# The output projection's weights: split during the input projection, kept in DRAM, loaded into place

## The chip, the cores and the metric

The kernel runs on one core of a Trainium2 chip. The metric is the device time of one execution in microseconds (us). The version before was run three times: 1436.47, 1436.74 and 1441.49 us, median 1436.74 us. The trace used here is of a further, profiled execution.

## The reference

One decoder layer in float32 on 1024 tokens of width 1024. The mixer projects the normalised tokens with one wide matrix `w_in`, runs sparse attention on part of the columns and a short convolution on another, normalises both results, concatenates them and multiplies by one matrix `w_out`. Cross-attention into 256 memory tokens and a SwiGLU block follow. Cut to the part at issue:

```python
def hybrid_mixer(h, w_in, w_out, gn_nsa, gn_conv, conv_w, rel_bias, ...):
    proj = h @ w_in
    q, kc, vc, ks, vs, kw, vw, gl, cb, cc, cx = jnp.split(proj, IN_SPLITS, axis=-1)
    ...
    o_nsa = nsa_attention(q, kc, vc, ks, vs, kw, vw, gates, ...)   # (S, 512)
    u = cc * cx
    y = sum(conv_w[k] * u_pad[:, CONV_K - 1 - k: CONV_K - 1 - k + S] for k in range(CONV_K))
    o_conv = cb * y                                                # (S, 512)
    merged = jnp.concatenate([rmsnorm(o_nsa, gn_nsa), rmsnorm(o_conv, gn_conv)], axis=-1)
    return merged @ w_out                                          # w_out: (1024, 1024)
```

## The kernel before

Every float32 matrix product is made of three products of float32r operands: a number is split into hi (its copy in float32r, written by ScalarE) and lo (the rest, a subtraction on VectorE or GpSimd), and `mm3` (lines 122 to 125) issues hi x hi, hi x lo and lo x hi.

The work runs in stages. **Input projection** (to about 306 us of the trace): `proj_t` takes 128 columns of `w_in` at a time. SyncE loads them (`wr`), ScalarE writes `wh`, GpSimd writes `wl`, both double-buffered, and TensorE makes 48 matmuls of 512 columns. Beside it `prep_step` (line 298) prepares four pieces of the cross-attention's weights, one call per projection: it loads a piece into the only `praw` tile, splits it into `phl` (two tiles) on ScalarE and VectorE, and lets GpSimd store the result to DRAM one call later. After the sixth projection `mem_norm` uses the same tiles. **Attention** (306 to 577 us): 32 tasks of two heads. The scores of a task go through VectorE (minimum and bias), ScalarE (exponentials) and GpSimd (weights times gates) and come back to TensorE as transposes and products. Between them stand 16 `fill` units, which multiply the convolution's half by rows 512 to 1023 of `w_out` (tiles `wos[4]` to `wos[7]`). **Middle** (577 to about 800 us): `u_proj` multiplies the attention's half by rows 0 to 511 (`wos[0]` to `wos[3]`), then come the norms and the cross-attention. The SwiGLU block follows.

`load_wo(k)` (line 196) fills `wos[k]`, 128 rows of `w_out` as hi and lo, in one of the six tiles named `big`: two loads of 256 KB into `wraw`, and for each half a copy on ScalarE and a subtraction on VectorE. For k below 4 the attention's norm gain (`cols`, 12 + k) is multiplied in by lines 205 and 206. It is called for 4 to 7 ahead of the last projection, for 0 and 1 at tasks 9 and 21, and for 2 and 3 behind the attention.

A scheduler with a timing model of its own places each instruction in its engine's order; the order is then fixed, and an engine works it off without overtaking. So a call's place in the program is not its place on the engines. SyncE issues DMAs on one queue, GpSimd on another.

Of the kernel before, what the change touches and what calls it, by code (L numbers as in the profile page):

```python
# [9 lines left out]
F32 = mybir.dt.float32  # L10
F32R = mybir.dt.float32r
AF = mybir.ActivationFunctionType
OP = mybir.AluOpType
# [53 lines left out]
def hymba_kernel(ctx: ExitStack, tc: tile.TileContext, a, out: bass.AP):  # L67
# [9 lines left out]
    def f(t):  # L77
        return t.bitcast(F32)

    def dram(name, shape, dt=F32):  # L80
        return dpool.tile(shape, dt, name=name)
# [88 lines left out]
    wq_d = [dram(f"wq_d{c}", [P, 2, D], F32R) for c in range(2)]  # L170
    wm_d = [dram(f"wm_d{k}", [P, 2, D], F32R) for k in range(2)]
    km_d = dram("km_d", [P, 2, MH, MEMN], F32R)
    vm_d = dram("vm_d", [P, 2, MH, P], F32R)
# [17 lines left out]
    def big_tile():  # L191
        return big.tile([P, 4, 512], F32, name="big")

    wos, wraw = {}, [None]

    def load_wo(k):
        wos[k] = t = big_tile().bitcast(F32R)
        for n in range(2):
            raw = wraw[0].tile([P, 512], F32, name="wraw")
            Y.dma_start(raw, a["w_out"][0, k * P:(k + 1) * P, n * 512:(n + 1) * 512])  # L200
            if k >= 4:
                split(t[:, n, :], t[:, 2 + n, :], raw, V)
            else:
                col = cols[:, 12 + k:13 + k]
                A.activation(t[:, n, :], raw, AF.Copy, scale=col)
                V.scalar_tensor_tensor(t[:, 2 + n, :], raw, col, f(t[:, n, :]), op0=OP.mult, op1=OP.subtract)


    with ExitStack() as st:
# [82 lines left out]
        for k in range(2):  # L292
            prep_q.append((a["mem_wq"][0, :, k * P:(k + 1) * P].rearrange("(k p) c -> p k c", p=P),
                           [cols[:, 20 + c:21 + c] for c in range(KT)], wq_d[k]))
            prep_q.append((a["mem_wo"][0, k * P:(k + 1) * P, :], None, wm_d[k]))
        prep_live, prep_done = [], []

# [23 lines left out]
        def proj_t(c0, post):  # L321
            wh, wl = load_w(wst, w_in[0, :, c0:c0 + P])
            prep_step()
            pss = [pmm.tile([P, 512], F32, name="mm") for _ in range(2)]
            for k in range(KT):
                for n in range(2):
                    tok = slice(n * 512, (n + 1) * 512)
                    mm3(pss[n], wh[:, k, :], wl[:, k, :], hh[:, k, tok], hl[:, k, tok], k == 0, k == KT - 1)
            for n in range(2):
                post(n, pss[n], slice(n * 512, (n + 1) * 512))  # L330
# [55 lines left out]
        with ExitStack() as s2:  # L386
            cp = pool(s2, "conv", side="right")
            for c in range(4):
# [18 lines left out]
                if c == 3:  # L407
                    mem_tr()
                proj_t(C_CX + c * P, post_cx)
                V.tensor_scalar(y, u[:, 2:S + 2], cols[:, c:c + 1], None, op0=OP.mult)  # L410
# [21 lines left out]

        mem_kv()
        conv_stat()
        prep_stack.close()
# [11 lines left out]

        wraw[0] = pool(st, "wr", bufs=2, side="right")

# [112 lines left out]

        for k in (4, 5):
            load_wo(k)
        for k in (6, 7):
            load_wo(k)
        proj_k("s", C_KS)


    wraw[0] = ap2 = pool(at_stack, "ap2", bufs=2)  # L570
    with ExitStack() as st:
# [57 lines left out]
        def soft_stage(n, i, h0, qi, mb, nt):  # L629
# [58 lines left out]
            for j in range(2):  # L688
                (V if i < 0 else Gp).tensor_scalar(psel[:, j, :W], psel[:, j, :W], sm[:, 0, j:j + 1], 1.0, op0=OP.mult, op1=OP.mult)
            soft[n] = psel, pwin, w0  # L690
# [91 lines left out]
        for n, (i, h0) in enumerate(tasks):  # L782
# [9 lines left out]
            for _ in ahead:  # L792
                pass
            if n in (9, 21):
                load_wo(int(n == 21))
            if h0 == H - 2:
# [8 lines left out]
        for m in range(FILL[NT], 2 * NT):  # L805
            fill(m)
        load_wo(2)
        load_wo(3)
        wq = []
# [615 lines left out]
```

## Time and profile before

| | |
|---|---|
| median of three runs | 1436.74 us |
| profiled execution, its own time | 1439.82 us |
| its span in the trace | 1438.0 us |
| TensorE (PE) busy | 1352.8 us, 94% |
| VectorE (DVE) busy | 946.9 us, 66% |
| ScalarE (ACT) busy | 683.7 us, 48% |
| GpSimd (POOL) busy | 488.5 us, 34% |
| mean granted TensorE clock | 0.976 |

PE is busy nearly all the time, so a change shows in the time where PE waits, or where its clock is granted at half. A timeline row gives start, length, engine, line, instruction, tiles, and in brackets how long the engine had been idle and what it waited for. PEclk is the granted clock: 1.00 is 2.4 GHz, 0.50 is 1.2 GHz.

### The profile page before, as it was taken

Reading aid. Unit: us, or ns where it says so; the run is one execution under the profiler, and the core shown is the slowest. Engines: PE = TensorE matmul, PEld = TensorE weight load, DVE = VectorE, ACT = ScalarE, POOL = GpSimd, SP = SyncE. Lnnn points to the kernel's source line nnn. Section 1 sums busy time; section 2 is a strip of 40 time slices with the busy share of each in tenths; the row PEclk is TensorE's granted clock in tenths of the full one; section 3 lists DMA queues with packets and bytes.
Section 4 is the critical chain, followed back from the end, with each engine's and each line's share of the span. In section 5 each row is a group of like instructions: output and inputs, shape, how many; then the busy total and the mean of one; then the engine's idle time right before and its main releaser. Section 6 shows DMA issues by size and latency. Waiting matters only on the chain.

```text
span 1438.0 us, 19770 instructions
## 1 busy us (share of the span) xinstructions
PE 1352.8 (94%) x6748; PEld 1127.4 (78%) x6748; DVE 946.9 (66%) x2079; ACT 683.7 (48%) x1473; POOL 488.5 (34%) x456
## 2 busy tenths in 40 slices
PE   8999999989999998898779789999999999989997
PEld 6988888878988897686658568888888887867885
DVE  6454543456899995478876786555544544898787
ACT  5432242437877796345775432333333333444463
POOL 1222231217767563111120666644445441000000
PEclk9999999989999999899989999999999999999999
DMA  7572266394633203843236455432222225930213
GB/s 227 153 239 76 74 217 203 117 184 101 113 66 67 45 8 131 315 152 100 107 96 214 123 152 166 145 119 80 89 84 85 81 88 206 378 112 30 67 59 118
DMA packets 159909, 186.50 MB, mean 130 GB/s; under 512 B 8402, under 2 KB 115070, under 8 KB 157599
## 3 DMA queue, kind: packets, MB, share of 16 engines
q1 hardware_dynamic: 129568, 146.44, 31.8%
q0 software_dynamic: 29088, 36.70, 10.5%
q10 hardware_dynamic: 1152, 2.10, 0.4%
q8 instruction: 53, 0.87, 0.3%
q14 instruction: 48, 0.39, 0.1%
HBM read 130.16 MB, written 55.05 MB: 129 GB/s over the span
## 4 chain that ended last, share of the span: by engine, by line
PE 43%; DVE 5%; issue 2%; ACT 0%; POOL 0%; DVEq 0%
PE m L125 13%; PE m L124 13%; PE m L123 13%; DVE al L120 1%; PE s L123 1%; PE s L124 1%; PE s L125 1%; DVE bl L120 1%; DVE big L120 0%; DVE q L1339 0%; PE o L125 0%; DVE T2l L120 0%; PE o L123 0%; DVE cb L1328 0%; PE o L124 0%
## 5 line engine op out<-in xcount | busy, mean ns | idle before, releaser
L119 ACT ACTIVATE ah<-raw 128x512 fp32r<-128x512 f32 x132 | 83.1, 631 | 209.1 <-PE m L124 192.5
L123 PE MATMUL mm<-hh,wh 128*128 128x512 f32 x320 | 125.8, 393 | 0.0
L124 PE MATMUL mm<-hl,wh 128*128 128x512 f32 x320 | 125.3, 392 | 0.0
L125 PE MATMUL mm<-hh,wl 128*128 128x512 f32 x320 | 124.8, 392 | 0.0
L120 DVE TENSOR_TENSOR al<-raw,ah 128x512 fp32r<-128x512 f32 x118 | 104.1, 884 | 25.8 <-ACT ah L119 25.6
L120 POOL TENSOR_TENSOR wl<-wr,wh 128x1024 fp32r<-128x1024 f32 x22 | 55.6, 2530 | 160.7 <-ACT wh L119 160.6
L124 PE MATMUL m<-bl,ah 128*128 128x512 f32 x264 | 102.8, 395 | 4.0 <-DVE bl L120 4.0
L125 PE MATMUL m<-bh,al 128*128 128x512 f32 x264 | 101.0, 393 | 4.8 <-DVE al L120 4.8
L1162 POOL TENSOR_TENSOR sg<-sg,tmp 128x512 f32<-128x512 f32 x44 | 66.0, 1501 | 82.5 <-DVE tmp L1161 39.5
L124 PE MATMUL m<-big,ah 128*128 128x512 f32 x232 | 92.0, 397 | 0.0
L120 DVE TENSOR_TENSOR ptl<-t,pth 128x512 fp32r<-128x512 f32 (+1 forms) x120 | 77.2, 655 | 11.7 <-ACT pth L119 11.5
L123 PE MATMUL m<-bh,ah 128*128 128x512 f32 x264 | 72.2, 390 | 1.1 <-ACT bh L119 1.1
L119 ACT ACTIVATE pth<-t 128x512 fp32r<-128x512 f32 (+1 forms) x120 | 66.5, 572 | 14.1 <-PE t L712 13.1
L125 PEld LDWEIGHTS mm<-hh,wl 128*128 128x128 f32 x320 | 60.5, 189 | 12.8 <-POOL wl L120 0.3
L123 PEld LDWEIGHTS mm<-hh,wh 128*128 128x128 f32 x320 | 60.4, 189 | 12.6
L124 PEld LDWEIGHTS mm<-hl,wh 128*128 128x128 f32 x320 | 60.5, 189 | 12.4
L124 PEld LDWEIGHTS m<-bl,ah 128*128 128x128 f32 x264 | 50.1, 190 | 16.4 <-DVE bl L120 6.0
L125 PEld LDWEIGHTS m<-bh,al 128*128 128x128 f32 x264 | 49.9, 190 | 16.2 <-DVE al L120 6.0
L1154 DVE TENSOR_TENSOR sg<-m,t 128x512 f32<-128x512 f32 x40 | 27.6, 691 | 49.7 <-PE m L125 43.4
L1185 POOL TENSOR_TENSOR s<-raw 128x512 f32<-128x512 f32 x22 | 29.3, 1333 | 89.8 <-DMA raw<-in_ffn_wu_dram 65.0
L1161 DVE TENSOR_TENSOR tmp<-m,t 128x512 f32<-128x512 f32 x40 | 27.6, 691 | 48.5 <-PE m L125 21.6
L123 PEld LDWEIGHTS m<-bh,ah 128*128 128x128 f32 x264 | 49.5, 188 | 11.9 <-ACT bh L119 1.6
(492 smaller groups left out, 4163.1 us busy)
## 6 DMA issues: line engine op xcount, KB each, us to landing
raw<-in_ffn_wg_dram SPq DMA_DIRECT2D x52, 256.0 KB, 3.2
raw<-in_ffn_wu_dram SPq DMA_DIRECT2D x52, 256.0 KB, 3.0
hid_d<-sg SPq DMA_DIRECT2D x22, 512.0 KB, 2.7
q<-in_ffn_wd_dram SPq DMA_DIRECT2D x44, 256.0 KB, 5.4
q<-hid_d SPq DMA_DIRECT2D x44, 256.0 KB, 5.1
wr<-in_w_in_dram SPq DMA_DIRECT2D x20, 512.0 KB, 3.9
x<-in_x_dram SPq DMA_DIRECT2D x16, 512.0 KB, 4.5
q_d<-big POOLq DMA_DIRECT2D x8, 1024.0 KB, 5.1
```

Source lines behind the costliest of these rows:

```text
L119: A.activation(hi, src, AF.Copy)
L120: (lo_eng or V).tensor_tensor(lo, src, f(hi), OP.subtract)
L123: T.matmul(ps, lh, rh, start=start, stop=False)
L124: T.matmul(ps, lh, rl, start=False, stop=False)
L125: T.matmul(ps, ll, rh, start=False, stop=stop)
L1154: V.tensor_tensor(dst, src0, src1, OP.add)
L1161: V.tensor_tensor(tmp, src0, src1, OP.add)
L1162: Gp.tensor_tensor(dst, dst, tmp, OP.mult)
L1185: Gp.tensor_tensor(s3, raw[w, "11"], raw[w, "21"], OP.subtract)
```

## The change

`w_out` goes through `prep_step` too: eight more pieces are loaded, split and stored in `wo_d` in DRAM, 4 to 7, 0 and 1 ahead of `mem_norm`, 2 and 3 behind `mem_tr`. `prep_step` is called twice per projection. `load_wo(k)` is now one load of 1 MB from `wo_d` into the `big` tile, issued by GpSimd. The loads of 2 and 3 are called at tasks 29 and 30, and those at tasks 9, 21, 29 and 30 are to stand behind the last weighting of their task on GpSimd. The `wraw` buffers go (two of 2 KB per partition in each of two pools).

```diff
--- before.py
+++ after.py
@@ -169,6 +169,7 @@
     oc_d = dram("oc_d", [P, 2, 4, S], F32R)
     wq_d = [dram(f"wq_d{c}", [P, 2, D], F32R) for c in range(2)]
     wm_d = [dram(f"wm_d{k}", [P, 2, D], F32R) for k in range(2)]
+    wo_d = [dram(f"wo_d{k}", [P, 2, D], F32R) for k in range(8)]
     km_d = dram("km_d", [P, 2, MH, MEMN], F32R)
     vm_d = dram("vm_d", [P, 2, MH, P], F32R)
     pc_d = [dram(f"pc_d{i}", [P, D]) for i in range(NT)]
@@ -191,19 +192,11 @@
     def big_tile():
         return big.tile([P, 4, 512], F32, name="big")
 
-    wos, wraw = {}, [None]
+    wos = {}
 
     def load_wo(k):
-        wos[k] = t = big_tile().bitcast(F32R)
-        for n in range(2):
-            raw = wraw[0].tile([P, 512], F32, name="wraw")
-            Y.dma_start(raw, a["w_out"][0, k * P:(k + 1) * P, n * 512:(n + 1) * 512])
-            if k >= 4:
-                split(t[:, n, :], t[:, 2 + n, :], raw, V)
-            else:
-                col = cols[:, 12 + k:13 + k]
-                A.activation(t[:, n, :], raw, AF.Copy, scale=col)
-                V.scalar_tensor_tensor(t[:, 2 + n, :], raw, col, f(t[:, n, :]), op0=OP.mult, op1=OP.subtract)
+        wos[k] = big_tile().bitcast(F32R)
+        Gp.dma_start(wos[k].rearrange("p a b -> p (a b)"), wo_d[k].rearrange("p x c -> p (x c)"))
 
 
     with ExitStack() as st:
@@ -293,6 +286,12 @@
             prep_q.append((a["mem_wq"][0, :, k * P:(k + 1) * P].rearrange("(k p) c -> p k c", p=P),
                            [cols[:, 20 + c:21 + c] for c in range(KT)], wq_d[k]))
             prep_q.append((a["mem_wo"][0, k * P:(k + 1) * P, :], None, wm_d[k]))
+
+        def prep_wo(k):
+            prep_q.append((a["w_out"][0, k * P:(k + 1) * P, :], None if k >= 4 else [cols[:, 12 + k:13 + k]], wo_d[k]))
+
+        for k in (4, 5, 6, 7, 0, 1):
+            prep_wo(k)
         prep_live, prep_done = [], []
 
         def prep_step():
@@ -320,6 +319,7 @@
 
         def proj_t(c0, post):
             wh, wl = load_w(wst, w_in[0, :, c0:c0 + P])
+            prep_step()
             prep_step()
             pss = [pmm.tile([P, 512], F32, name="mm") for _ in range(2)]
             for k in range(KT):
@@ -406,6 +406,8 @@
                 proj_t(C_CC + c * P, post_cc)
                 if c == 3:
                     mem_tr()
+                    prep_wo(2)
+                    prep_wo(3)
                 proj_t(C_CX + c * P, post_cx)
                 V.tensor_scalar(y, u[:, 2:S + 2], cols[:, c:c + 1], None, op0=OP.mult)
                 for k in (1, 2):
@@ -431,6 +433,7 @@
             V.tensor_copy(rc, rsqrt(prp, ps, 512, NT, "gc"))
 
         mem_kv()
+        assert not (prep_q or prep_live or prep_done)
         conv_stat()
         prep_stack.close()
 
@@ -445,7 +448,6 @@
 
             proj_t(c0, post_k)
 
-        wraw[0] = pool(st, "wr", bufs=2, side="right")
 
         with ExitStack() as s2:
             cp = pool(s2, "cmp", side="right")
@@ -560,14 +562,12 @@
         zb = ap1.tile([P, NBLK], F32, name="zb")
         Gp.memset(zb, 0.0)
 
-        for k in (4, 5):
-            load_wo(k)
-        for k in (6, 7):
+        for k in range(4, 8):
             load_wo(k)
         proj_k("s", C_KS)
 
 
-    wraw[0] = ap2 = pool(at_stack, "ap2", bufs=2)
+    ap2 = pool(at_stack, "ap2", bufs=2)
     with ExitStack() as st:
         ap3 = pool(st, "ap3", bufs=2, side="right")
         pss = pool(st, "pss", bufs=3, space=PSUM)
@@ -686,7 +686,7 @@
             for j in range(2):
                 (Gp if i < 8 else V).tensor_scalar(pwin[:, j, :WW], pwin[:, j, :WW], sm[:, 1, j:j + 1], 1.0, op0=OP.mult, op1=OP.mult)
             for j in range(2):
-                (V if i < 0 else Gp).tensor_scalar(psel[:, j, :W], psel[:, j, :W], sm[:, 0, j:j + 1], 1.0, op0=OP.mult, op1=OP.mult)
+                last["norm"] = Gp.tensor_scalar(psel[:, j, :W], psel[:, j, :W], sm[:, 0, j:j + 1], 1.0, op0=OP.mult, op1=OP.mult)
             soft[n] = psel, pwin, w0
 
         def pv_stage(i, h0, pc, psel, pwin, w0):
@@ -791,8 +791,9 @@
                     next(ahead, None)
             for _ in ahead:
                 pass
-            if n in (9, 21):
-                load_wo(int(n == 21))
+            if n in (9, 21, 29, 30):
+                with tc.issue_after(last["norm"].ins):
+                    load_wo((9, 21, 29, 30).index(n))
             if h0 == H - 2:
                 sq = ap2.tile([P, 4, P], F32, name="sq", bufs=1)
                 A.activation(sq, ons[i], AF.Square)
@@ -804,8 +805,6 @@
                     fill(m)
         for m in range(FILL[NT], 2 * NT):
             fill(m)
-        load_wo(2)
-        load_wo(3)
         wq = []
         for c in range(2):
             wq.append(big_tile().bitcast(F32R).rearrange("p a b -> p (a b)"))
```

The scheduler then places things anew. TensorE's order in the projections stays the same up to the last two of them. Three other places:

VectorE at the start of the attention. `ks` is the last projection's result, `s` the first scores, `cnm` their minima, `wraw` the rows of `w_out`. Before:

```order
L120 TENSOR_TENSOR ks<-mm,ks 64x512 x4
L206 SCALAR_TENSOR_TENSOR big<-wraw,cols,big 128x512 x2
L591 ISA pc,cnm<-s,ct 128x64
...
L648 ISA pwin,nm<-s,wb 128x128
L648 ISA nm 128x1
L593 TENSOR_TENSOR pc<-cnm,pc 128x512
L206 SCALAR_TENSOR_TENSOR big<-wraw,cols,big 128x512
```

and now:

```order
L120 TENSOR_TENSOR ks<-mm,ks 64x512 x4
L591 ISA pc,cnm<-s,ct 128x64
...
L648 ISA pwin,nm<-s,wb 128x128
L648 ISA nm 128x1
L593 TENSOR_TENSOR pc<-cnm,pc 128x512
L648 ISA pwin,nm<-s,wb 128x128
```

The four rows of line 206, for `wos[0]` and `wos[1]`, are gone from there.

ScalarE at the end of the attention: `pth` are hi copies of the last task's transposes, `on` its output, `sq`, `gny` its norm, `mh` the hi copies for `u_proj`. Before:

```order
L205 ACTIVATE big<-wraw,cols 128x512 x2
L774 ACTIVATE stg<-f,rc 128x512
L119 ACTIVATE pth<-t 128x512
L205 ACTIVATE big<-wraw,cols 128x512
L119 ACTIVATE pth<-t 128x512 x2
L205 ACTIVATE big<-wraw,cols 128x512
L119 ACTIVATE pth<-t 128x512 x2
L119 ACTIVATE pth<-t 128x256
L728 ACTIVATE otmp<-o 64x512 x2
L798 ACTIVATE sq<-on 128x512
L119 ACTIVATE mh<-on 128x512 x2
L108 ACTIVATE gny<-gnv 128x1
```

and now:

```order
L774 ACTIVATE stg<-f,rc 128x512
L119 ACTIVATE pth<-t 128x512 x3
L119 ACTIVATE pth<-t 128x256
L728 ACTIVATE otmp<-o 64x512 x2
L799 ACTIVATE sq<-on 128x512
L108 ACTIVATE gny<-gnv 128x1
L109 ACTIVATE gny<-gny 128x1
L119 ACTIVATE mh<-on 128x512 x3
```

The copies of line 205 are gone, and `mh` stands behind `gny`.

ScalarE in the third to sixth projection: `wh` is a projection's hi weight, `phl<-praw` a prepared piece, line 343 `mem_norm`. Before:

```order
L119 ACTIVATE phl<-praw 128x1024
L119 ACTIVATE wh<-wr 128x1024
L343 ACTIVATE phl,ssq<-phl 128x1024
L108 ACTIVATE prey<-prev 128x1
L343 ACTIVATE phl,ssq<-phl 128x1024
L109 ACTIVATE prey<-prey 128x1
L119 ACTIVATE wh<-wr 128x1024
```

and now:

```order
L119 ACTIVATE phl<-praw 128x1024 x2
L119 ACTIVATE wh<-wr 128x1024
L418 ACTIVATE big<-oc,cols 128x1024
L424 ACTIVATE sqc<-oc 128x1024
L119 ACTIVATE phl<-praw 128x1024
L396 ACTIVATE big<-mm 128x512
L119 ACTIVATE wh<-wr 128x1024
L396 ACTIVATE big<-mm 128x512
L119 ACTIVATE phl<-praw 128x1024
L310 ACTIVATE phl<-praw,cols 128x1024
L119 ACTIVATE wh<-wr 128x1024
L310 ACTIVATE phl<-praw,cols 128x1024
```

One or two pieces now stand ahead of each `wh`, and `mem_norm` follows later.

On GpSimd the loads of `wos[2]` and `wos[3]` stand behind the last `mhl` load and directly ahead of the two loads of `wq`.

## Rows read from the trace of the kernel before

**Rows 1.** Windows by stage: busy us (instructions) per engine, clock, DMA share, GB/s.

```profile
core 0: us, PE busy (x) PEld busy (x) DVE busy (x) ACT busy (x) POOL busy (x), PEclk, DMA share, GB/s
100.00:200.00 100.00, 100.00 (x504) 85.27 (x503) 46.18 (x46) 26.23 (x37) 29.93 (x15) 1.00 0.37 109
...
300.00:400.00 100.00, 92.64 (x574) 82.43 (x573) 68.76 (x319) 69.77 (x193) 57.86 (x87) 0.93 0.69 126
```

**Rows 2.** Timeline, start of the attention: start, us, engine, line, operation, tiles, [idle before].

```profile
306.86 2.71 DVE L120 TENSOR_TENSOR ks<-mm,ks 64x512 fp32r<-64x512 f32 x4 [4.14 <-ACT ks L119]
...
311.17 1.33 ACT L205 ACTIVATE big<-wraw,cols 128x512 fp32r<-128x512 f32 x2 [2.32 <-DMA wraw<-in_w_out_dram]
311.92 1.41 DVE L206 SCALAR_TENSOR_TENSOR big<-wraw,cols,big 128x512 fp32r<-128x512 f32 x2 [2.35 <-ACT big L205]
...
314.09 0.48 PE L642 MATMUL s<-kw,qi 128*128 128x128 f32 x1 [4.58 <-DVE cnm L591]
...
315.64 0.73 PE L123 MATMUL f<-big,mhl 128*128 128x512 f32 x1
...
320.42 0.39 PE L125 MATMUL f<-big,mhl 128*128 128x512 f32 x1
...
320.59 1.04 POOL L598 TENSOR_TENSOR pc<-pc,csm 128x512 f32<-128x512 f32 x1 [17.12 <-DVE sm L685]
...
332.91 0.50 PE L123 MATMUL f<-big,mhl 128*128 128x512 f32 x1 [1.91 <-DMA mhl<-oc_d]
```

**Rows 3.** Windows of 4 us around that wait.

```profile
310.00:314.00 4.00, 0.00 (x0) 0.00 (x0) 2.05 (x11) 1.33 (x2) 0.00 (x0) 0.52 0.29 84
314.00:318.00 4.00, 3.91 (x12) 3.29 (x13) 2.69 (x19) 1.56 (x3) 0.00 (x0) 0.50 0.39 126
```

**Rows 4.** Timeline, end of the attention.

```profile
569.22 0.50 PE L718 MATMUL o<-pth,vst 128*128 128x256 f32 x2 [0.55 <-ACT pth L119]
...
573.43 0.72 ACT L205 ACTIVATE big<-wraw,cols 128x512 fp32r<-128x512 f32 x1 [3.77 <-DMA wraw<-in_w_out_dram]
...
574.68 0.50 PE L718 MATMUL o<-pth,vst 128*128 128x256 f32 x2 [2.92 <-ACT pth L119]
...
580.69 1.13 ACT L119 ACTIVATE mh<-on 128x512 fp32r<-128x512 f32 x2
580.84 1.87 PE L801 MATMUL f<-ones,sq 128*128 128x1 f32 x8 [3.58 <-ACT sq L798]
...
583.16 0.20 ACT L109 ACTIVATE gny<-gny 128x1 f32<-128x1 f32 x1
```

**Rows 5.** Timeline, the prepared pieces and the projections' weights.

```profile
59.75 0.34 SPq L318 DMA_DIRECT2D praw<-in_mem_wo_dram  x1
...
64.10 1.06 ACT L119 ACTIVATE phl<-praw 128x1024 fp32r<-128x1024 f32 x1 [7.02 <-DMA praw<-in_mem_wo_dram]
65.19 1.23 DVE L120 TENSOR_TENSOR phl<-praw,phl 128x1024 fp32r<-128x1024 f32 x1 [5.47 <-ACT phl L119]
66.45 0.37 SPq L318 DMA_DIRECT2D praw<-in_mem_wq_dram  x1
...
78.37 1.06 ACT L119 ACTIVATE phl<-praw 128x1024 fp32r<-128x1024 f32 x1 [4.75 <-DMA praw<-in_mem_wo_dram]
...
84.54 2.60 DVE L412 SCALAR_TENSOR_TENSOR big<-u,cols,big 128x1024 f32<-128x1024 f32 x2
...
90.01 1.06 ACT L343 ACTIVATE phl<-phl 128x1024 f32<-128x1024 f32 x1 [9.63 <-DMA phl<-in_mem_dram]
...
93.74 3.48 POOL L120 TENSOR_TENSOR wl<-wr,wh 128x1024 fp32r<-128x1024 f32 x1 [9.80 <-ACT wh L119]
...
119.92 2.41 POOL L120 TENSOR_TENSOR wl<-wr,wh 128x1024 fp32r<-128x1024 f32 x1 [8.04 <-ACT wh L119]
...
130.81 2.39 POOL L120 TENSOR_TENSOR wl<-wr,wh 128x1024 fp32r<-128x1024 f32 x1 [6.41 <-ACT wh L119]
```

**Rows 6.** DMA issues: tiles, queue, count, KB each, median us to landing.

```profile
big<-wq_d POOLq DMA_DIRECT2D x2, 1024.0 KB, 7.3
```

## The prediction

> **What bounds the kernel now.** I read the engines' busy shares on the page first: TensorE (PE) works 1352.8 of 1438.0 us, so 85.2 us of PE's waiting is all there is to win, beside the time in which its clock is granted at half. The windows by stage come next. During the projections PE is busy in all 100 of 100 us, and VectorE (DVE) 46, ScalarE (ACT) 26 and GpSimd (POOL) 30 [rows 1]: work added to those three costs nothing there unless it makes a weight late. From 300 to 400 us PE is busy 92.64, at a clock of 0.93 on average [rows 1]: 7.4 us of waiting, and about 7 us' worth of clock. The timeline shows where. At the attention's start PE waits 4.58 us until 314.09 for `cnm` [rows 2], and the clock is 0.52 from 310 to 314 and 0.50 from 314 to 318 [rows 3]. At the attention's end PE waits 0.55, 2.92 and 3.58 us [rows 4]. The long waits that the change touches are at these two places, about 7 us together; the rest lies in stages that it leaves as they are, but for small changes of order.
>
> **Start of the attention.** The DVE subtraction of `ks` ends at 306.86 + 2.71 = 309.57. The next thing in DVE's order is L206, which needs ACT's L205, and that waits for the `wraw` load until 311.17; L206 runs to 311.92 + 1.41 = 313.33, then `cnm` is made, and PE goes on at 314.09, 0.76 us behind L206 [rows 2]. Both lines go. DVE can begin L591 at 309.57, and PE by the same 0.76 at about 310.3: 3.8 us earlier. Behind that stand 12 `fill` matmuls, from 315.64 to 320.42 + 0.39 = 320.81, that is 5.2 us [rows 2] at a clock of 0.50 [rows 3]. If the shorter pause leaves the clock at full, they take half, and 2.6 us more are won: 6.4 in all. The gain stays only if the chain behind comes earlier as well. POOL starts L598 at 320.59, having waited 17.12 us for DVE's `sm`; the `mhl` load for the fill at 332.91, for which PE still waits 1.91 us, is issued on the same queue [rows 2]. DVE reaches `sm` earlier by the 3.8, by the 2.6 if PE's fills take half, and by 0.7 for one more L206 that is gone from between (half of 1.41): 7.1 us at most, and the fill can follow by 6.4. Bounds: -3.8, if the clock is at half all the same, and -7.1. I take **-6.4**, since the clock at 1.00 is what the neighbouring stage has [rows 1] with PE busy throughout.
>
> **End of the attention.** ACT waits 3.77 us for `wraw` and copies it from 573.43 to 574.15; only then come the `pth` copies, and PE has waited 2.92 us when it goes on at 574.68 [rows 4]. Without L205 the copy itself (574.68 - 574.15 = 0.5) remains of the wait: 2.4 us gone, and of the 0.55 at 569.22, which has the same cause, all: -2.9. Against this, `mh` moves behind `gny` on ACT. Before, `mh` runs at 580.69, and PE is through with the norm's sums at 580.84 + 1.87 = 582.71. Now it starts when `gny` ends, 583.16 + 0.20 = 583.36 [rows 4], and the first of its copies, half of 1.13, is there at 583.9: PE's `u_proj` begins 1.2 us later. Sum **-1.7**. Bounds: -3.5 if `mh` finds its way without delay (both waits whole), +1.2 if other work fills the waits on ACT. The loads of `wos[2]` and `wos[3]` stand on POOL ahead of those of `wq`, which are as large and land in 7.3 us [rows 6]; each pushes `wq` back by up to that, and `wq` is not needed until `u_proj` is done. I cost this at nothing; it is hidden by `u_proj`.
>
> **Projections.** Eight pieces more cost ACT 1.06 and DVE 1.23 us each [rows 5], in engines that have room [rows 1]. What counts is the chain of the one `praw` tile: load issued at 59.75, copy at 64.10 (4.35 us later), subtraction 65.19 to 66.42, next load 66.45 [rows 5], a cycle of 6.7 us. A projection takes 130.81 - 119.92 = 10.89 us [rows 5]. So two pieces (13.4) don't fit in one projection, but the order of ACT puts fewer than that ahead of each `wh` on average. The tightest place is the first: the old fourth piece is copied at 78.37; the next one's copy is done early, but its subtraction stands on DVE behind the convolution's products, which end at 84.54 + 2.60 = 87.14 [rows 5]. So: subtraction to 88.4, load, copy at 88.4 + 4.35 = 92.75 to 93.8, `wh` to 94.9, `wl` to 97.3 with 2.41 us, as at 119.92, or to 98.4 with the 3.48 of 93.74. Before, this `wl` ended at 93.74 + 3.48 = 97.22 [rows 5], and PE was not late then. PE would wait 0.1 to 1.2 us. I take **+1.2**, the row nearest in place, and keep 0 to +3: up to 1.4 us more if a load lands a third later than 4.35. The last place is a `wl` made at 119.92, needed about a period later, at 130.8. Its piece, six cycles behind 78.37, is copied at 118.6, and with copy, `wh` and `wl` (1.06 + 1.06 + 2.41 = 4.5) all is ready at 123.1: 7.7 us to spare. The splits of `wos[4]` to `wos[7]` ahead of the last projection went beside a busy PE; their going brings nothing.
>
> What the row shows of `wl` is 3.48 us at 93.74 and 2.41 and 2.39 later, the same instruction on the same shapes [rows 5]. The Trainium skill (page "SBUF — State Buffer", section "Who interferes with whom") says that a VectorE instruction with two inputs in SBUF holds up a GpSimd instruction that reads SBUF, for the whole of it. By that rule the added subtractions, each 1.23 us with both inputs in SBUF, speak against the change: each that meets a `wl` makes it up to 1.2 us longer. The difference of 1.07 in the trace agrees with it. By the rule this term is 1.2, without it 0.1; the choice above is made by the row at 93.74.
>
> **Attention and middle.** Of the 7.4 us of waiting from 300 to 400 [rows 1], 2.8 lie outside the wait at 314.09. Small changes of order there can win or lose that much: **0**, bounds -3 and +3. The loads into `big` are 1 MB instead of 512 KB for each `wos`; the DMA share is 0.69 in that stretch [rows 1], and no engine's work depends on them for tens of us, except at the end.
>
> **Sum.** -6.4 - 1.7 + 1.2 + 0 = -6.9. The profiled execution took 1439.82 us (1.82 beside its span), which would become 1432.9. It is 3.08 above the median of 1436.74, and I take the difference to be one of runs: 1436.74 - 6.9 = **1429.8 us**.
>
> **Rivals.** *Half of the gain.* At the start another wait takes the place, or the clock falls all the same: DVE had waited 4.14 us for ACT's `ks` copy already [rows 2], and a PE that waits there loses clock without L206. Then -3.8; and if at the end `wos[3]` comes late by a few tenths or `mh` costs its 1.2 with nothing won, the sum is -3.8 + 1.2 + 1.2 = -1.4, or with the end's gain -3.8 - 1.7 + 1.2 = -4.3: 1432.4 to 1435.3. For it: the clock was at 0.52 in the whole of 310 to 314 [rows 3]. Against it: PE's wait of 4.58 is far the longest there.
>
> *Slower: the chain of `praw` is too slow.* The loads share the DMA engines with those of `wr` and of `mem`: ACT's L343 waited 9.63 us for `mem` until 90.01 [rows 5], some 9.3 after the subtraction (1.09 + 1.23 behind the copy at 78.37) had freed the tiles. With a landing of 9.3 instead of 4.35 the cycle is 11.7; the last piece is copied at 78.37 + 6 x 11.7 = 148.6, `wl` is done at 153.1, and PE has waited 22.3 us. Sum -6.4 - 1.7 + 22.3 = +14.2: 1450.9 us. It decides from a landing of 7.0 on (a cycle of 9.4, 8.5 us of stall, which eats the gain); slower by 0.5% it is from 8.1 on. Against it: the wait of 9.63 was for several loads at once, a piece of half a MB alone took 4.35, and the DMA engines are busy 0.37 in that stage [rows 1].
>
> *More gain.* The `wl` isn't late (0), the start gives 7.1, the end 1.7, and the freed ACT and DVE work in the attention takes 2.8 from the waits there: -11.6, 1425.1 us. For it: DVE and ACT are both on the way of each softmax, and eight copies and subtractions between tasks go. Against it: they had been placed by the same scheduler.
>
> *The change does nothing where I look*, since another wait ends last at both places: 1436.7.
>
> **How the numbers follow.** Forecast 0.45, within 1426.5 and 1432.5; half of the gain 0.18; nothing 0.04; slower 0.09; more gain 0.24. The range of 1423.5 to 1438.5 holds the forecast, most of the two cases on either side and the bounds of the unknown terms (-3 further down, +3 and a wait at the end further up); outside are the slow chain and a tail below, 0.15 to 0.2 together. What a measurement of this kernel tells from no change is 0.5%, 7.2 us: faster means under 1429.6, which cuts the forecast nearly in half. Faster 0.21 + 0.24 = 0.45; slower 0.09; within 0.5% 0.46.
>
> **What would show it.** Right: after `ks`, PE goes on within 1.5 us of the subtraction's end; the clock near 318 is 1.00 and the first 12 fill matmuls stand 0.22 us apart; POOL's L598 comes some 7 us earlier against `ks`. At the end no wait of 2.9 on `pth`, but one of about a microsecond on `mh`. In the projections one wait of about a microsecond at the fifth weight. Wrong: a clock of 0.5 beside the first fills, a second wait of several us in the first two tasks, waits of PE on `wl` or `wh` in each projection from 97 to 155, or `wos[2]` and `wos[3]` named as what `u_proj` waits for.

## The result

The changed kernel took 1428.66 us (median of 6 runs, 1425.5 to 1433.65) against 1439.75 for the kernel before (6 runs): a ratio of 0.9926, with an interval from 0.991 to 0.9943. That is 8 to 13 us faster, by the middle 10.6. The profiled execution took 1429.11 us, its span is 1427.3, and TensorE (PE) is busy 1349.8 us of it. The forecast was a gain of 6.9 us and a time of 1429.8, so the time lies in the range that was given; but several terms of the sum were off, in opposite directions, as the trace shows.

**Stages.** The windows by stage of the changed kernel (columns as in [rows 1] and [rows 3]):

```profile
core 0: us, PE busy (x) PEld busy (x) DVE busy (x) ACT busy (x) POOL busy (x), PEclk, DMA share, GB/s
100.00:200.00 100.00, 97.68 (x467) 81.54 (x466) 52.62 (x53) 33.54 (x47) 30.87 (x19) 0.98 0.66 217
300.00:400.00 100.00, 97.47 (x615) 87.12 (x615) 71.06 (x327) 71.01 (x199) 61.10 (x91) 0.97 0.68 123
...
314.00:318.00 4.00, 3.20 (x10) 2.60 (x11) 3.61 (x26) 1.90 (x7) 0.00 (x0) 0.59 0.26 32
318.00:326.00 8.00, 8.00 (x37) 6.65 (x36) 3.11 (x26) 3.24 (x12) 5.46 (x9) 0.78 0.09 33
```

The projections, where PE never waited, now have 2.3 us of waiting and a DMA share of 0.66 instead of 0.37. From 300 to 400 us, 2.5 us of PE's time are waits instead of 7.4. The clock behind the first scores is still near half.

**Start of the attention**, timeline, to be held against [rows 2]:

```profile
313.91 0.30 PE L642 MATMUL s<-kw,qi 128*128 128x128 f32 x1 [0.51 <-DVE ks L120]
315.12 0.47 PE L642 MATMUL s<-kw,qi 128*128 128x128 f32 x1 [0.80 <-DVE cnm L591]
...
316.25 0.74 PE L123 MATMUL f<-big,mhl 128*128 128x512 f32 x1
...
318.50 1.04 POOL L598 TENSOR_TENSOR pc<-pc,csm 128x512 f32<-128x512 f32 x1 [11.85 <-DVE csm L597]
...
321.06 0.63 PE L125 MATMUL f<-big,mhl 128*128 128x512 f32 x1
...
332.31 0.50 PE L123 MATMUL f<-big,mhl 128*128 128x512 f32 x1 [1.01 <-DMA mhl<-oc_d]
```

The first scores are late: 313.91, in the trace of before 309.09. Behind them the wait of 4.58 us [rows 2] is one of 0.80. The 12 fill matmuls take as long as before, 0.43 us apart from 316.25 to 321.06. GpSimd (POOL) reaches L598 4.6 us behind the first scores instead of 11.5; in the trace of before, two more L206 stood on VectorE (DVE) ahead of the chain that leads to it. The rows of before:

```profile
309.09 0.30 PE L642 MATMUL s<-kw,qi 128*128 128x128 f32 x1 [0.51 <-DVE ks L120]
...
316.62 0.75 DVE L206 SCALAR_TENSOR_TENSOR big<-wraw,cols,big 128x512 fp32r<-128x512 f32 x1 [1.20 <-ACT big L205]
...
317.91 0.75 DVE L206 SCALAR_TENSOR_TENSOR big<-wraw,cols,big 128x512 fp32r<-128x512 f32 x1
```

**Projections.** Where PE waits in them, timeline:

```profile
117.40 2.53 POOL L120 TENSOR_TENSOR wl<-wr,wh 128x1024 fp32r<-128x1024 f32 x1 [5.73 <-ACT wh L119]
...
119.98 0.50 PE L125 MATMUL mm<-hh,wl 128*128 128x512 f32 x1 [0.47 <-POOL wl L120]
...
126.67 2.04 SPq L340 DMA_DIRECT2D phl<-in_mem_dram  x2
...
138.43 1.06 ACT L343 ACTIVATE phl<-phl 128x1024 f32<-128x1024 f32 x1 [1.50 <-DMA phl<-in_mem_dram]
...
140.63 1.05 ACT L119 ACTIVATE wh<-wr 128x1024 fp32r<-128x1024 f32 x1
141.77 5.66 POOL L120 TENSOR_TENSOR wl<-wr,wh 128x1024 fp32r<-128x1024 f32 x2 [12.11 <-ACT wh L119]
141.85 3.35 DVE L344 SCALAR_TENSOR_TENSOR phl<-phl,prey,praw 128x1024 f32<-128x1024 f32 x1
...
144.16 0.79 PE L125 MATMUL mm<-hh,wl 128*128 128x512 f32 x1 [1.70 <-POOL wl L120]
```

`mem_norm` (L343), pushed back by six pieces, waits for its own load, and a projection's `wh` stands behind it on ScalarE (ACT): PE waits 1.70 us at 144.16. Its row there lasts 0.79 instead of 0.50; the clock from 144 to 148 us is 0.57. The two waits make 2.2 of the 4.8 us by which the first scores are late; 1.7 more is clock, and the projections started 0.4 us later.

**End of the attention**, ACT, POOL, SyncE (SP) and PE, against [rows 4]:

```profile
560.67 1.24 POOL L199 DMA_DIRECT2D big<-wo_d  x2 [7.63 <-PE f L125]
562.06 0.53 POOL L811 DMA_DIRECT2D big<-wq_d  x1
562.76 0.53 POOL L811 DMA_DIRECT2D big<-wq_d  x1 [0.18 <-issue]
...
563.69 0.45 SPq L865 DMA_DIRECT2D on<-on_d  x1
...
566.01 0.44 SPq L865 DMA_DIRECT2D on<-on_d  x1
...
570.59 1.77 PE L802 MATMUL f<-ones,sq 128*128 128x1 f32 x8 [3.58 <-ACT sq L799]
...
572.82 0.20 ACT L109 ACTIVATE gny<-gny 128x1 f32<-128x1 f32 x1
573.96 0.63 ACT L119 ACTIVATE mh<-on 128x512 fp32r<-128x512 f32 x1 [0.93 <-DMA on<-on_d]
579.17 0.63 ACT L119 ACTIVATE mh<-on 128x512 fp32r<-128x512 f32 x1 [4.58 <-DMA on<-on_d]
579.85 0.80 PE L123 MATMUL p<-big,mh 128*128 128x512 f32 x1 [7.49 <-ACT mh L119]
```

PE reaches the norm's sums at 570.59 instead of 580.84, then waits 7.49 us for `mh`. ACT is not late behind `gny`; it waits for `on`, two loads of 256 KB that `u_proj` reads back from DRAM. They are issued at 563.69 and 566.01, right behind four loads of 1 MB by GpSimd, and are there 10 and 13 us later.

**All kernels by stage**, in us, from the timelines: first projection product to the end of the last; first scores to the end of the last `pth`/`ptl` product; from there to `u_proj`'s first product; to the first product of the SwiGLU part; to its last. For the attention, PE's waits and what the clock took (PE's busy time times one minus the granted clock) are added up over windows of 10 us. The first scores are counted from the start of the trace; where the projections start scatters too, from 53.0 to 54.5 us.

```
kernel        projections  attention (waits, clock)  to u_proj  middle  SwiGLU  first scores
before           253.2      268.1 (17.8, 6.0)           5.3      220.6   626.4     309.1
before_again     251.4      268.2 (20.2, 4.2)           5.3      217.8   627.1     308.5
changed          257.6      253.1 ( 7.7, 3.1)          12.8      216.8   622.1     313.9
after_again      256.3      252.6 ( 7.7, 3.1)          13.0      218.5   623.1     312.5
only01           253.3      258.7 (11.6, 3.6)           6.7      219.9   625.8     309.0
only23           253.0      267.6 (15.8, 9.0)          10.4      217.5   625.8     308.8
only4567         254.6      271.3 (18.5,10.1)           5.3      218.2   626.2     311.6
preponly         254.7      268.2 (19.2, 5.5)           5.3      220.6   625.9     311.9
four             257.1      252.7 ( 7.7, 3.1)          12.7      215.0   621.9     313.9
wqlate           256.1      253.4 ( 8.0, 3.1)           5.7      215.8   624.4     312.3
p0123            251.5      253.6 ( 8.3, 3.1)          13.1      215.8   623.4     308.4
p0123wq          251.7      253.5 ( 8.3, 3.1)           5.9      217.4   624.9     308.7
hold01           254.6      266.5 (16.1, 5.3)           5.3      218.2   626.9     311.5
h01p23wq         253.2      261.1 (12.3, 4.7)           5.8      216.9   620.4     308.9
```

Against before, the change loses 4.4 us in the projections, wins 15.0 in the attention, loses 7.5 ahead of `u_proj` and wins 8.1 behind it.

The projections hold clock that is not the change's. Windows of 12 us in which PE never waits, first of hold01, which prepares no piece, then of before_again:

```profile
222.00:234.00 12.00, 12.00 (x55) 10.59 (x55) 2.85 (x5) 2.47 (x4) 2.35 (x1) 0.72 0.80 253
222.00:234.00 12.00, 12.00 (x70) 10.53 (x70) 2.98 (x5) 2.67 (x5) 2.34 (x1) 1.00 0.75 241
```

This stretch costs 3.4 us of clock in hold01 and nothing in before_again. In each of the fourteen traces it costs about 0, 1.7 or 3.4 us: nothing in before_again, p0123 and p0123wq, 1.7 in before and in the changed kernel, 3.4 in after_again, preponly, only4567 and wqlate. So up to 3.4 us between two projection stages of the table are scatter.

### The profile page after: what moved, and what is told of

The parts are those of the page before. It is cut to its first block, busy times and chain, and to the rows that moved or that the text cites. A ratio compares the mean times of both kernels' runs of the same rounds, so it can differ in the third digit from the quotient of the medians.

```text
span 1427.3 us, 19754 instructions
## 1 busy us (share of the span) xinstructions
PE 1349.8 (95%) x6748; PEld 1127.1 (79%) x6748; DVE 940.2 (66%) x2071; ACT 682.6 (48%) x1465; POOL 497.2 (35%) x472
## 4 chain that ended last, share of the span: by engine, by line
PE 75%; DVE 12%; issue 4%; DMA 4%; ACT 3%; POOL 1%; SPq 0%; DVEq 0%; POOLq 0%; ACTq 0%
PE m L125 13%; PE m L124 13%; PE m L123 13%; PE mm L125 4%; PE mm L123 4%; PE mm L124 4%; PE o L718 3%; PE t L712 2%; DVE ptl L120 1%; PE s L642 1%; PE s L643 1%; DVE psel L659 1%; PE mm L228 1%; PE tr L485 1%; PE p L123 1%
## 5 line engine op out<-in xcount | busy, mean ns | idle before, releaser
L120 DVE TENSOR_TENSOR al<-raw,ah 128x512 fp32r<-128x512 f32 x118 | 107.1, 908 | 24.8 <-ACT ah L119 24.8
```

The costliest lines, as they stand in the source:

```text
L120: (lo_eng or V).tensor_tensor(lo, src, f(hi), OP.subtract)
```

## The experiments

**How far one trace can be trusted.** The two kernels once more, unchanged.

> The kernel before, profiled once more. Theory 1 (the 8 us that the change won behind u_proj, between 582 us and the end, belong to the program: a changed order of instructions): a second trace of before shows the same stage lengths as the first within 1 us each (attention's first scores at about 309, u_proj's first product at about 582.5, SwiGLU's wait on al at about 808, last m product at about 1398). Rival (these 8 us are scatter between executions, such as the clock): the stages from 582 on differ by 3 us or more from the first trace.

> The changed kernel, profiled once more. Theory 1 (its 1.70 us wait on wl at 144 hangs on the landing of mem_norm's loads, which scatters by some 2 us between executions, while the wait of 7.5 us on mh belongs to the program): first scores between 311.5 and 314.5, the wait on mh 7 to 8 us again. Rival (both are fixed): first scores at 313.9 within 0.5 us.

Measured: before 1437.3 us, changed 1429.96. The table's second and fourth rows: stages repeat within 3 us, the attention within 0.5. Of the parts behind `u_proj` the middle moved by 2.8 us and the SwiGLU part by 0.7, so theory 1's bound of 1 us was too narrow, and the rival does not hold either. So the attention's 15 us and the 7.5 ahead of `u_proj` belong to the programs; of the 8 behind `u_proj`, 2 to 3 are scatter. The projections of the changed kernel were 1.3 us shorter the second time, with waits of 0.66 and 0.49 instead of 0.47 and 1.70. The second load of `mem_norm` was there at 136.88 instead of 138.43, so some 1.2 us of the last wait hang on when a load lands, as theory 1 had it; a wait of half a microsecond at each of the two places came again. The wait on `mh` was 7.51.

**One part alone: 0 and 1.**

```diff
+        if k in (0, 1):
+            Gp.dma_start(t.rearrange("p a b -> p (a b)"), wo_d[k].rearrange("p x c -> p (x c)"))
+            return
...
+        for k in (0, 1):
+            prep_wo(k)
```

`prep_step` is called twice per projection, and the two loads are held behind the norms of tasks 9 and 21, as in the change.

> Only wos[0] and wos[1] are prepared in the projections and loaded straight; 2 to 7 are loaded and split as before. Theory 1 (the gain at the attention's start comes from these two alone, and two pieces cost the projections next to nothing): no wait of PE on wl in the projections, PE's wait on cnm at the attention's start under 1.5 us instead of 4.58, fill 2 some 5 us earlier against the first scores than before, sum -5 us, give or take 4 us for a changed order elsewhere (ratio 0.9965). Rival (the start is freed only with all eight, since the rest of the wraw work moves into its place): the wait on cnm stays over 3 us, 0 to -2 us.

Measured: 1429.58 us, ratio 0.9929 (0.9917 to 0.9942): nearly the whole gain of the change by two pieces of eight. The wait on `cnm` is 0.81 us and no weight is late; one product still waits 3.30 us for `pth`:

```profile
310.22 0.48 PE L654 MATMUL s<-kw,qi 128*128 128x128 f32 x1 [0.81 <-DVE cnm L603]
...
564.78 0.51 PE L730 MATMUL o<-pth,vst 128*128 128x256 f32 x2 [3.30 <-ACT pth L119]
```

The attention is 9.4 us shorter, not 5: 4.3 are won by the first fill, the rest up to the end. Waits behind it that the prediction took for fixed go with it, such as 1.65 us on `nm` at 484 (a row of 484.13 in before's timeline), since the order behind was placed anew. (In the changed kernel that wait is gone too, but one of 1.48 us on `ptl` at 481 is there.)

**One part alone: 2 and 3.** As above with `if k in (2, 3)`, and the loads at tasks 29 and 30.

> Only wos[2] and wos[3] are prepared and loaded straight (behind the norm of tasks 29 and 30), the others as before. Theory 1 (PE's waits on pth at the attention's end go, but four loads of 1 MB stand in front of u_proj's token loads): no wait of PE on pth over 1 us behind the last scores, the square's sums 4 to 7 us earlier against the last scores, then a wait of PE on mh of 5 to 8 us; u_proj within 1.5 us of where it was, sum 0, give or take 4 us for a changed order. Rival (the late mh has another cause than these loads): mh is on time and the sum is -5 us.

Measured: 1441.03 us, ratio 1.0005 (0.9996 to 1.0014), as theory 1 said. In the trace, where the last scores end at 547.81 (before: 543.18):

```profile
575.63 0.51 PE L732 MATMUL o<-ptl,vst 128*128 128x256 f32 x2 [0.17 <-DVE ptl L120]
579.94 1.79 PE L818 MATMUL f<-ones,sq 128*128 128x1 f32 x8 [3.57 <-ACT sq L815]
586.73 0.79 PE L123 MATMUL p<-big,mh 128*128 128x512 f32 x1 [5.00 <-ACT mh L119]
```

No wait on `pth` is left, and 5.00 us on `mh` are there instead. From the end of the last scores the norm's sums come after 32.1 us instead of 37.7, and `u_proj` after 38.9 instead of 39.4: won and given back at the same place.

**One part alone: 4 to 7.** As above with `if k in (4, 5, 6, 7)`.

> Only wos[4] to wos[7] are prepared and loaded straight; 0 to 3 are loaded and split as before. Theory 1 (these four bring nothing, since their splits ahead of the attention were beside a busy PE; four more pieces in the projections cost 0 to 4 us, by how the chain of praw falls): wait on cnm 4 to 6 us as before, attention 266 to 269 us, ratio 1.000 to 1.003. Rival (their going frees the start, since wraw of 0 and 1 is loaded earlier): the wait on cnm is under 2 us and the ratio 0.996 or less.

Measured: 1442.08 us, ratio 1.0005 (0.9989 to 1.0022); the wait on `cnm` is 5.01 us. These four alone bring nothing. The attention, 3 us longer in this trace, had more time at the lower clock (10.1 us).

**The price of preparing.** All eight pieces are prepared and stored, but nothing reads them; every `load_wo` is the old one.

> All eight pieces are prepared and stored as in the changed kernel, but every wos is still loaded and split from w_out as before, so the stored pieces are not used. Theory 1 (the 4.8 us by which the attention starts later are the price of the eight pieces): attention's first scores at 313 to 314.5 instead of 309.1, with PE waits on wl near 120 and 144; the rest as before, sum +4 to +5 us, give or take 4 us for a changed order (ratio 1.003). Rival (the pieces are hidden, and the delay comes from the missing splits of wos[4] to [7] or the order around them): first scores at 309 to 310, sum 0.

Measured: 1439.12 us, ratio 0.9994 (0.9981 to 1.0007). Theory 1's +4 to +5 fell: there is no wait of PE in the projections at all, although the pieces stand in the same order. (The first scores come at 311.9, between the two expectations; 1.7 of the 2.8 us against before is the clock that scatters, and 1.3 the later start of the projections.) `mem_norm`'s loads were issued at 126.25, in the changed kernel at 126.67, but the second landed 2.2 us earlier, at 136.2 instead of 138.4:

```profile
126.25 2.08 SPq L348 DMA_DIRECT2D phl<-in_mem_dram  x2
...
136.22 1.06 ACT L351 ACTIVATE phl<-phl 128x1024 f32<-128x1024 f32 x1 [1.58 <-DMA phl<-in_mem_dram]
...
138.42 1.05 ACT L119 ACTIVATE wh<-wr 128x1024 fp32r<-128x1024 f32 x1
139.56 2.38 POOL L120 TENSOR_TENSOR wl<-wr,wh 128x1024 fp32r<-128x1024 f32 x1 [10.25 <-ACT wh L119]
139.63 3.39 DVE L352 SCALAR_TENSOR_TENSOR phl<-phl,prey,praw 128x1024 f32<-128x1024 f32 x1
```

By after_again (136.88, and a wait of 0.49) the landing accounts for some 1.2 of the 1.70 us. The other half microsecond, and the 0.47 at 119.98, come again in both other traces with this order (after_again 0.66 and 0.49, wqlate 0.48 and 0.24). In those three the projections start at 53.5 or 53.6 us, in preponly at 54.5, so that PE needs each weight 0.9 us later there. So the pieces use up the slack: a microsecond of start or of landing then decides whether PE waits.

**Taking two pieces out of the way.**

```diff
-        for k in (4, 5, 6, 7, 0, 1):
+        for k in (4, 5, 6, 7):
...
-                    prep_wo(2)
-                    prep_wo(3)
+                    for k in range(4):
+                        prep_wo(k)
+                    prep_step()
+                    prep_step()
```

> The changed kernel, but pieces 0 and 1 are prepared behind mem_tr with 2 and 3, so that only four new pieces stand ahead of mem_norm; TensorE's order is the same as in the changed kernel. Theory 1 (the projections lose some 4.4 us because the chain of the one praw tile pushes mem_norm, and with it the eighth weight, too far back): no wait of PE on wl in the projections, first scores at 309 to 310 instead of 313.9, the rest as in the changed kernel, 4 to 5 us faster than it (about 1424.5, ratio to before 0.9895). Rival (the DMA traffic and the shared engines slow the weights, wherever the pieces stand): waits of 2 us remain and the attention starts at 312 or later, as fast as the changed kernel.

Measured: 1428.56 us, ratio 0.9911 (0.9895 to 0.9927), no faster than the changed kernel. The waits on `wl` are gone, as theory 1 said, but the attention starts at 313.9 all the same: a piece (L310), which waits for its load, now stands on ACT ahead of the convolution's statistics, and PE waits there.

```profile
192.59 1.15 ACT L310 ACTIVATE phl<-praw,cols 128x1024 fp32r<-128x1024 f32 x1 [4.98 <-DMA praw<-in_w_out_dram]
...
197.38 2.21 DVE L429 TENSOR_TENSOR sqc<-sqc,oc 128x1024 f32<-128x1024 f32 x1 [0.80 <-ACT oc L428]
199.74 1.92 PE L434 MATMUL tr<-ones,sqc 128*128 128x1 f32 x16 [1.54 <-DVE sqc L429]
```

With one of 0.44 us at 202.90 the waits make 2.0 us, as much as in the changed kernel. The waits on `wl` hang on the place of the pieces, as theory 1 had it; the remedy only moved the wait.

**The loads of `wq` later.**

```diff
+                    last["on"] = Gp.tensor_tensor(ons[i][...], tmp[...], tmp[...], OP.add)
...
+            with tc.issue_after(last["on"].ins):
+                Gp.dma_start(wq[c], wq_d[c].rearrange("p x c -> p (x c)"))
```

`issue_after` puts the loads behind the named instruction in GpSimd's order.

> The changed kernel, but the two loads of wq are issued by GpSimd behind its last addition of on, so that only the loads of wos[2] and wos[3] stand in front of u_proj's token loads; the scheduler then puts the copies mh directly behind the square again. Theory 1 (PE's wait of 7.49 us on mh comes from 4 MB of loads that the 256 KB token loads share the DMA engines with): the wait shrinks to 0 to 3 us, 4 to 7 us faster than the changed kernel (about 1423, ratio to before 0.988), if nothing waits for wq later. Rival 1 (the token loads are late for another reason, their own queue): the wait stays over 6 us, no gain. Rival 2 (wq is late in its turn): a new wait of the same size at the cross-attention's first product of h2, no gain.

Measured: 1420.38 us, ratio 0.9852 (0.9836 to 0.9868), 8 us faster than the changed kernel and than four, which was timed beside it, and the lowest median of all:

```profile
559.44 1.24 POOL L199 DMA_DIRECT2D big<-wo_d  x2 [7.71 <-PE f L125]
567.13 1.49 POOL L730 TENSOR_TENSOR on<-otmp 64x256 f32<-64x256 f32 x2 [6.45 <-ACT otmp L728]
568.57 1.11 POOL L812 DMA_DIRECT2D big<-wq_d  x2
...
570.76 0.63 ACT L119 ACTIVATE mh<-on 128x512 fp32r<-128x512 f32 x1 [0.96 <-DMA on<-on_d]
...
571.44 0.79 PE L123 MATMUL p<-big,mh 128*128 128x512 f32 x1 [1.06 <-ACT mh L119]
```

The wait on `mh` is 1.06 us. The second token load, issued at 564.76, is there at 570.76, 6 us later instead of 13. The loads on SyncE's own queue, a `pt` load of 512 KB between the two token loads, are the same in both, so theory 1 holds against rival 1. The copies `mh` also stand ahead of `gny` again; but in p0123 and in the changed kernel they wait for the DMA, not for `gny`, so the loads are the cause. Nothing waits for `wq` later: of rival 2 there is no sign.

**Without 4 to 7, and both together.** p0123 prepares 0 to 3 only; p0123wq is the same with `wq` late.

> The kernel before with the pieces 0 to 3 alone prepared and loaded straight (0 and 1 ahead of mem_norm, 2 and 3 behind mem_tr); 4 to 7 are loaded and split ahead of the last projection as before. Theory 1 (4 to 7 bring nothing and cost the projections their delay): first scores at 309 to 310, attention to its end as short as in the changed kernel (253 us from the first scores to the last product of pth), the wait on mh of 5 to 7.5 us as there; 4 us faster than the changed kernel (about 1424.5, ratio 0.9895). Rival (taking 4 to 7 out of the front of the attention is part of the gain): the attention is 3 us or more longer than in the changed kernel, no gain over it.

> As p0123, with the two loads of wq behind the last addition of on as well. Theory 1 (both losses of the changed kernel are separate and both go): first scores at 309 to 310, wait on mh 0 to 3 us, about 1419 to 1421 (ratio 0.986), the fastest. Rival (one of the two comes back in another place, as waits for wq or a changed order with new waits in the attention): 1424 or more.

Measured: p0123 1426.26 us, ratio 0.9894 (0.9879 to 0.9909). Projections 251.5 us, attention 253.6, and 7.68 us of waiting on `mh`:

```profile
574.49 0.63 ACT L119 ACTIVATE mh<-on 128x512 fp32r<-128x512 f32 x1 [4.55 <-DMA on<-on_d]
575.17 0.79 PE L123 MATMUL p<-big,mh 128*128 128x512 f32 x1 [7.68 <-ACT mh L119]
```

Leaving out 4 to 7 costs the attention nothing. p0123wq took 1422.09 us, ratio 0.9871 (0.9853 to 0.9889): the stages up to `u_proj` add up to the least in the table, but as timed it can't be told from wqlate. Of the 4.4 us that its profile has fewer in the projections, 3.4 are the clock that scatters, which its other runs need not have spared; they are not seen in the median. By its runs (1420.96 to 1425.57) the expected 1419 to 1421 was too low.

**Place or work?** Nothing is prepared; the raw loads for 0 and 1 are issued by GpSimd behind the norms of tasks 9 and 21, so that the scheduler moves their splits out of the attention's start.

```diff
-            Y.dma_start(raw, a["w_out"][0, k * P:(k + 1) * P, n * 512:(n + 1) * 512])
+            (Gp if k < 2 else Y).dma_start(raw, a["w_out"][0, k * P:(k + 1) * P, n * 512:(n + 1) * 512])
...
             if n in (9, 21):
-                load_wo(int(n == 21))
+                with tc.issue_after(last["norm"].ins):
+                    load_wo(int(n == 21))
```

> The kernel before without any prepared piece; the raw loads for wos[0] and wos[1] alone are issued by GpSimd behind the norms of tasks 9 and 21, so that the scheduler places their copies and subtractions there instead of at the attention's start. Theory 1 (what the change won at the attention's start is the place of this work and its wait for a load, not the work itself): as only01, the wait on cnm under 1.5 us, attention some 9 us shorter, 1429 to 1431 us (ratio 0.993). Rival (the work itself costs: eight instructions of 0.7 us on ACT and DVE in the middle of two tasks, with PE waiting there): half of it or less, 1434 us or more.

> hold01 with pieces 2 and 3 alone prepared (behind mem_tr) and loaded straight, and the wq loads behind the last addition of on. Theory 1 (place, not preparation, for 0 and 1; preparation for 2 and 3, where no later place exists; wq late): first scores at 308 to 309.5, attention 253 to 256 us, u_proj within 3 us of the square's sums, 1420 to 1424 us, as wqlate and p0123wq. Rival (the split work in tasks 9 and 21 disturbs the tasks): attention 258 us or more, 1426 us or more.

Measured: hold01 1434.28 us, ratio 0.9951 (0.9935 to 0.9967): 7 us against only01's 10, between the two expectations, and by its time at the rival's bound.

```profile
312.69 0.48 PE L642 MATMUL s<-kw,qi 128*128 128x128 f32 x1 [0.80 <-DVE cnm L591]
```

From the first scores to the first fill it takes 2.3 us, as in only01, and 6.5 before; so all that was won up to the first fill is a matter of place. The rest of only01's gain isn't there: the splits now stand in tasks 9 and 21, and ahead of the last scores PE waits 11.0 us in hold01, and 11.0 again in h01p23wq, against 5.5 in only01. That the splits make these waits is likely but not shown: the order of all the tasks differs as well, and hold01's profiled execution was the slowest of its 12. h01p23wq took 1423.93 us, ratio 0.989 (0.9864 to 0.9916), with 261.1 us of attention: theory 1 held for the time, the rival for the attention. The two meet by a SwiGLU part of 620.4 us, the shortest of all, which neither had forecast.

## Why the prediction was right, and where it was not

The sign came out, and the mechanism named for the start and for the `pth` waits. The nearness of the time, 1428.66 against 1429.8, is in part luck. The gain was 10.6 us against 6.9: the forecast set out from a median of 1436.74, which six runs put at 1439.75. And the gain came by terms that erred against each other.

- **Start, -6.4 forecast.** At 332 us the changed kernel is 5.4 us earlier against the first scores (0.6 earlier, with a start 4.8 later). The step that the wait goes with L205 and L206 holds: 0.80 is left of 4.58, and hold01 shows that moving those lines is enough. POOL's L598 comes 6.9 us earlier by the same measure (forecast: up to 7.1), but not by the 2.6 of faster fills that the forecast put into this: two L206 and a wait of 1.20 us went from DVE's order behind the first scores' minima, where it had counted one L206. Wrong is the step "if the shorter pause leaves the clock at full, they take half": the clock is 0.59 and 0.78, and the fills are 0.43 us apart as before. In its place came the shorter wait for `mhl`, 1.01 instead of 1.91, and by the first fill only 4.2 us are won. The clock was already down in that stretch with only 0.51 and 0.80 us of waiting ahead of it. In every trace of the table the first fills stand 0.43 us apart; in before_again, after_again, four and wqlate the last four stand 0.23 apart.
- **Attention, 0 forecast.** It became 15.0 us shorter in all, where the start and the `pth` waits as forecast make 9.3. 13.0 of it are waits (10.1) and clock (2.9). Up to the end of the last scores (543.18 before, 540.38 now) 7.6 us are won, 5.4 of them by 332 us: that leaves some 2 us for this term, within its bounds of 3. The other 7.4 lie behind the last scores. By the totals only01 and only23 give 9.4 and 0.5, so the parts don't seem to add up; but only23's 0.5 is 5.5 won behind the last scores and 4.9 lost ahead of them, 3.0 us of it by a lower clock in its one trace.
- **End, -1.7 forecast.** The waits on `pth` went as forecast; with smaller ones, PE waits 0.6 us behind the last scores up to the last such product, instead of 5.3. But from the last scores to `u_proj` it takes 39.5 us now and 39.4 before: the gain forecast here is nil. What replaced the waits was wrong by mechanism: not `gny` (1.2 us), but the token loads. The step that failed is "I cost this at nothing; it is hidden by `u_proj`". It asked who waits for `wq`, not what other loads are in flight with it. To `u_proj` it costs 7.5 us; wqlate takes back all but 0.4 of it, and there the way from the last scores is 32.4 us.
- **Projections, +1.2 forecast.** 4.4 us in the first trace and 3.1 in the second, above the bounds of 0 to 3; by PE's waits alone 2.2 and 1.2. The forecast place, the fifth weight, was on time: `wl` took 2.49 us there (a row of 94.80), so the contention cost 0.1, not 1.2. The waits are two and four weights later, at the seventh and the ninth. The chain of `praw` was replayed only to its last piece; `mem_norm`, which follows it in the same tiles with three loads and has a `wh` behind it, was not in the sum. The rest is clock, 3.4 us in both traces, of which the trace of before has 1.7. In the first trace half of it follows the wait of 1.70 us; the other half, and all of it in the second, lies near 225 to 230 us, where it scatters whatever the kernel.
- **Middle and SwiGLU, 0 forecast.** 8.1 us shorter by the two first traces, 5.7 by the means of two each. Some 2.4 of this is scatter. About 4 us stand in the SwiGLU part, which is 622 to 623 in the changed kernel, four and p0123, and 624 to 625 in wqlate and p0123wq: PE's wait of 2.9 us on `T2l`, there in before, is gone in the changed kernel and back in wqlate. A late `u_proj` is not what decides it: only23 has one and keeps the wait (625.8), and h01p23wq, whose `u_proj` is not late, has the shortest part of all (620.4). It may be a matter of the order in which the scheduler put TensorE's products there; no run here isolates it, and it stays open.

Of the rivals, "more gain" had the right total but not the way: waits of attention did go, and the `wl` was late. The slow chain of `praw` stayed far from its 22 us.

## What to carry to other kernels

Before a load is costed at nothing, list what other loads are in flight with it, and which of those ends last: here 2 MB that nobody needed until u_proj was done held up 256 KB that PE waited for, and one edit of the issue order gave 8 us, where the whole change had given 11. A part that stands where the critical engine waits can be moved instead of removed; try the move first, and change the parts one by one, since two pieces of eight gave as much as all of them. When a scheduler places everything anew, stages without an edited line move as well, here by some 6 us of 846. Take a second trace of the same kernel before explaining a stage, and look at the granted clock in it: up to 3.4 us of the projections came and went with it.

## What the hardware did that was not expected

- Small loads beside large ones: a 256 KB load that was there after 6 us with 2 MB of GpSimd's loads ahead of it (wqlate) took 13 with 4 MB (the changed kernel, where further loads by GpSimd followed from 569.82), and the one before it 10.
- A VectorE instruction that started just behind a GpSimd one lasted until 1.1 us after its end: L352 of preponly, 1.28 us at 138.24, lasts 3.39 at 139.63, while `wl` runs on GpSimd from 139.56 to 141.94. It is nearly the time left of `wl` (2.31) and its own together. The Trainium skill (page "SBUF — State Buffer", section "Who interferes with whom") says that a VectorE instruction with two inputs in SBUF contends with a GpSimd instruction that reads SBUF, and that the ports they share are an exclusive lock; this row agrees, with VectorE as the one that waits. The prediction had looked only at the other direction.
- The same loads, issued 0.4 us apart in two programs with the same pieces ahead of them, were there 2.2 us apart (138.43 and 136.22). With a start of the projections 0.9 us apart, that decided whether PE waits.
- The granted clock fell with no wait of PE before it: near 224 to 230 us, at or just behind 32 products of 8 columns (L537 of before), in eleven of the fourteen traces, though PE was busy without a break. How long it stayed at half differed between executions of one kernel, 0.86 on average over 222 to 234 us in before and 1.00 in before_again.
